# Layer 1's attention weights: the division by the row sums moves from VectorE into the transpose on TensorE

## The chip, the cores and the metric

The kernel runs on one core of a Trainium2 chip. The metric is the device time of one execution in microseconds (us). Before the change three runs took 2331.3, 2332.67 and 2340.88 us, so the median is 2332.67 us. One more execution was recorded by the hardware profiler and gave all the rows below.

## The reference

The reference is a two-layer trunk on 1024 tokens of width 1024 in float32. Layer 0 has differential attention beside a convolution module, layer 1 has a state-space block beside multi-head latent attention, and each layer ends in a gated feed-forward part. The change touches the attention of layer 1 alone:

```python
def block(i, qb):
    sc = jnp.einsum('bqhd,bkhd->bhqk', qb, k, preferred_element_type=f32) * scale
    p = jax.nn.softmax(jnp.where(chunk_causal_mask(i, s), sc, -jnp.inf), axis=-1)
    return jnp.einsum('bhqk,bkhd->bqhd', p.astype(v.dtype), v)
```

There are six heads, `q` and `k` have 128 + 64 columns, `v` has 128, and the mask lets a query see all keys up to the end of its own chunk of 64. The softmax divides each row of exponentials by its sum.

## The kernel before

Layer 1's attention is `attn1` (from L966 on). It loops over six heads `h` and, in each, two halves `hf` of 512 queries. For each (head, half) `sm1` makes the weights and, one step later, `pv1` multiplies them with the values. So the order in which the work is written is: weights of step n, then (in the first half of a head) the loads and splits of the next head, then values of step n-1.

`sm1` works through four query blocks `jj` of 128 rows. A block has n = 128 to 1024 keys, because of the causal mask: half 0 has blocks of 128 to 512 keys and half 1 blocks of 640 to 1024. TensorE makes the scores in PSUM (`pss`, five products for each bank of 512 keys, L1038). Then `softmax_exp` follows: VectorE masks a corner (L344) and copies the negated scores to SBUF while it takes their extreme (L345), ScalarE takes the exponential in place and its row sum `sm` (L346). Then VectorE takes the reciprocal of the sum (L1041) and multiplies the block's weights by it, in place (L1042).

`pv1` calls `pv`, which layer 0 uses too. For each block `i` of 128 keys it transposes up to four 128x128 blocks of weights on TensorE into a PSUM tile `trp` (L365). ScalarE rounds them to the high part of `pt` (L369), VectorE takes the rest as the low part (L370), and three products per key block go into `po` (L115). GpSimd clears a corner of `pt` once in each `pv` (L368). A `pv` of half 0 has 10 transposed blocks and one of half 1 has 26, so the six heads have 6 x 36 = 216.

Around this, GpSimd splits the next head's operands (`bl`, L977, four of 128x1024 for each head), ScalarE makes their high parts (L976), and 192 products of the output projection (`psw`, L115 out of `w_out_first`) stand at the end of the program text as work without a hurry. The program is written with a tile framework: a planner simulates the whole kernel with its own costs and fixes the order of the instructions on every engine from that, so what stands late in the text can be issued early where an engine would be idle. Each engine then runs its list in order and waits at semaphores. Buffers: `pss` has two, `trp` two, `pt` three, the weights `wt` one for each half.

Of the kernel before, what the change touches and what calls it, by code (L numbers as in the profile page):

```python
# [10 lines left out]
F32 = mybir.dt.float32  # L11
# [3 lines left out]
ALU = mybir.AluOpType  # L15
# [5 lines left out]
P = 128  # L21
# [14 lines left out]
class Trunk:  # L36
# [315 lines left out]
            r.append((b, max(w, 256)))  # L352
        return r

    def pv(self, hf, Wt, offs, V, pool):
        nc = self.nc
        o = self.pp.tile([P, HALF], F32, tag="o", name="po", bufs=1)
        ni = 4 * hf + 4
        for i in range(ni):
            j0 = max(0, i - 4 * hf)  # L360
            lo = min(j0 * P, 256)
            pt = pool.tile([P, 2, HALF], F32R, tag="pt", name="pt", bufs=3)
            tr = self.pp.tile([P, HALF], F32, tag="tr", name="trp")
            for jj in range(j0, 4):
                nc.tensor.transpose(tr[:, jj * P:(jj + 1) * P], Wt[:, offs[jj] + i * P:offs[jj] + (i + 1) * P], self.ident)  # L365
            v = slice(j0 * P, HALF)
            if j0 * P > lo:
                nc.gpsimd.memset(pt[:, :, lo:j0 * P].bitcast(F32), 0.0)  # L368
            nc.scalar.copy(pt[:, 0, v], tr[:, v])  # L369
            nc.vector.tensor_tensor(pt[:, 1, v], tr[:, v], pt[:, 0, v].bitcast(F32), op=ALU.subtract)  # L370
            self.mm3(o[:, lo:HALF], (V[0][:, i, :], V[1][:, i, :]), (pt[:, 0, lo:HALF], pt[:, 1, lo:HALF]), i == 0, i == ni - 1)
        return o
# [648 lines left out]
    def sm1(self, h, hf, ops, V, pool):  # L1021
        nc = self.nc
        qh, ql, kh, kl, rh, rl, mr = ops
        scale = 192 ** -0.5
        tot = sum((4 * hf + jj + 1) * P for jj in range(4))
        Wt = pool.tile([P, tot], F32, tag=f"w{hf}", name="wt", bufs=1)
        offs, off = [], 0
        for jj in range(4):
            j = 4 * hf + jj
            n = (j + 1) * P  # L1030
            js = slice(j * P, (j + 1) * P)
            mx = self.small.tile([P, 1], F32, tag="mx1", name="mx1")
            sm = self.small.tile([P, 1], F32, tag="sm1", name="sm1")
            ps = self.pp.tile([P, S], F32, tag="big", name="pss")
            for b0, bw in self.banks(n):
                ks = slice(b0, b0 + bw)
                for a, b, first, last in ((qh, kh, True, False), (qh, kl, False, False), (ql, kh, False, False), (rh, mr, False, False), (rl, mr, False, True)):
                    nc.tensor.matmul(ps[:, ks], a[:, js], b[:, ks], start=first, stop=last)  # L1038
            w = Wt[:, off:off + n]
            self.softmax_exp(ps, n, mx, scale, w, sm)  # L1040
            nc.vector.reciprocal(sm, sm)  # L1041
            nc.vector.tensor_scalar(w, w, sm, None, op0=ALU.mult)  # L1042
            offs.append(off)
            off += n
        return h, hf, Wt, offs, V

    def pv1(self, st, Y0, Y1, pool):
        h, hf, Wt, offs, V = st
        o = self.pv(hf, Wt, offs, V, pool)
        dst = Y0[:, 2 + h, :] if h < 2 else Y1[:, h - 2, :]  # L1050
        self.nc.scalar.copy(dst[:, hf * HALF:(hf + 1) * HALF], o)

# [480 lines left out]
```

## Time and profile before

| what | before |
|---|---|
| median of three runs | 2332.67 us |
| profiled execution, its own time | 2335.67 us |
| profiled execution, span from first to last instruction | 2333.9 us |
| TensorE busy | 2155.4 us, 92% |
| VectorE busy | 1583.1 us, 68% |
| GpSimd busy | 1275.4 us, 55% |
| ScalarE busy | 945.6 us, 41% |
| mean granted TensorE clock | 0.970 |

The attention of layer 1 lies between about 1366 and 1590 us of the span. A TensorE matmul's end is modelled, so its duration holds pipeline latency; what one costs in a stream is the distance from its start to the next start. A float32 product is recorded as two matmuls where the operation is an ordinary one, and a transpose as one. "Granted clock" 1.00 is the 2.4 GHz level of TensorE, 0.50 the 1.2 GHz level.

### The profile page before, as it was taken

How to read it: one execution, taken by the hardware profiler on the slowest of the kernel's cores; microseconds unless marked ns; L12 is line 12 of the kernel's file. 1: busy time of each engine (PE TensorE's matmuls, PEld its weight loads, DVE VectorE, ACT ScalarE, POOL GpSimd, SP SyncE). 2: the span in 40 equal slices, each digit the busy share in tenths (PEclk: the TensorE clock that was granted, in tenths of full speed). 3: DMA queues.
4: the chain of work that ended last, by engine and by line, in shares of the span. 5: the costliest groups of instructions: out<-in, count | busy, mean ns of one | idle time of the engine just before them, and what ended most of it. 6: DMA issues, size and time to landing. Idle time of an engine off the chain costs nothing.

```text
span 2333.9 us, 27188 instructions
## 1 busy us (share of the span) xinstructions
PE 2155.4 (92%) x9684; PEld 1744.8 (75%) x9684; DVE 1583.1 (68%) x2175; ACT 945.6 (41%) x1413; POOL 1275.4 (55%) x740
## 2 busy tenths in 40 slices
PE   7999888888999999799979888999899999989997
PEld 5887667677788878578758667877688888867876
DVE  6859567689747865487874478756964444437778
ACT  5554556454222322333344346654532323224332
POOL 4997202135665566687654455421565656558864
PEclk9999999999999999899989998999899999999999
DMA  5134673244232333645442674324432323255444
GB/s 207 67 109 140 169 201 113 89 155 129 92 118 97 123 129 109 213 161 163 137 154 75 198 224 137 118 79 161 136 124 75 131 73 131 73 181 186 156 129 143
DMA packets 150664, 315.33 MB, mean 135 GB/s; under 512 B 20225, under 2 KB 43905, under 8 KB 150529
## 3 DMA queue, kind: packets, MB, share of 16 engines
q1 hardware_dynamic: 150528, 313.60, 41.6%
q8 instruction: 76, 1.25, 0.2%
q14 instruction: 60, 0.48, 0.1%
HBM read 214.39 MB, written 96.01 MB: 133 GB/s over the span
## 4 chain that ended last, share of the span: by engine, by line
PE 68%; DVE 13%; DMA 6%; issue 5%; POOL 4%; ACT 3%; SPq 1%; POOLq 0%; DVEq 0%; ACTq 0%
PE b L115 30%; PE psd L115 13%; PE psw L115 6%; PE psc L115 5%; PE psq L115 3%; PE po L115 2%; PE pss L1038 2%; POOL wl L1123 2%; PE trp L365 1%; DVE hl L1253 1%; DVE acc L1271 1%; DMA bm<-k_s 1%; PE psv L115 1%; PE psu L115 1%; DMA hr<-l_h_s 1%
## 5 line engine op out<-in xcount | busy, mean ns | idle before, releaser
L1123 POOL TENSOR_TENSOR wl<-raw,wh 128x1024 fp32r<-128x1024 f32 (+1 forms) x238 | 621.3, 2616 | 399.0 <-ACT wh L1121 387.1
L115 PE MATMUL b<-T,wh 128*128 128x512 f32 x1408 | 438.6, 393 | 3.1 <-DVE F L1172 3.1
L1121 ACT CAST wh<-raw 128x1024 fp32r<-128x1024 f32 (+1 forms) x238 | 241.9, 1023 | 430.3 <-PE b L115 266.1
L115 PE MATMUL b<-B,wh 128*128 128x512 f32 x1056 | 335.2, 398 | 13.8 <-DVE c L1163 10.4
L115 PEld LDWEIGHTS b<-T,wh 128*128 128x128 f32 x1408 | 263.9, 188 | 63.1 <-issue 3.7
L115 PE MATMUL psd<-wh,hh 128*128 128x512 f32 x616 | 248.3, 404 | 42.3 <-ACT hh L1252 20.3
L115 PE MATMUL b<-T,wl 128*128 128x512 f32 x704 | 276.6, 393 | 2.3 <-POOL wl L1123 2.1
L115 PEld LDWEIGHTS b<-B,wh 128*128 128x128 f32 x1056 | 201.6, 191 | 60.3 <-ACT B L1089 7.0
L115 PE MATMUL psd<-wl,hh 128*128 128x512 f32 x616 | 245.9, 400 | 0.0
L115 PE MATMUL psd<-wh,hl 128*128 128x512 f32 x616 | 234.5, 400 | 2.2 <-DVE hl L1253 2.2
L1271 DVE TENSOR_TENSOR acc<-acc,psd 128x512 f32<-128x512 f32 (+1 forms) x208 | 178.1, 884 | 73.1 <-PE psd L115 73.1
L115 PE MATMUL b<-B,wl 128*128 128x512 f32 x528 | 209.4, 397 | 4.2 <-POOL wl L1123 4.2
L115 PE MATMUL psw<-wh,jt 128*128 128x512 f32 x512 | 175.5, 408 | 17.1 <-ACT jt L488 9.6
L1172 DVE TENSOR_TENSOR p<-p,b 128x1024 f32<-128x1024 f32 (+1 forms) x88 | 83.5, 950 | 138.1 <-PE b L115 128.1
L1252 ACT CAST hh<-hr 128x1024 fp32r<-128x1024 f32 (+1 forms) x84 | 82.2, 980 | 233.9 <-PE psd L115 200.3
L115 PEld LDWEIGHTS psd<-wh,hh 128*128 128x128 f32 x616 | 118.8, 193 | 76.4 <-ACT hh L1252 26.3
L1253 DVE TENSOR_TENSOR hl<-hr,hh 128x1024 fp32r<-128x1024 f32 (+1 forms) x84 | 148.8, 1775 | 17.5 <-DMA hr<-l_h_s 10.8
L115 PEld LDWEIGHTS b<-T,wl 128*128 128x128 f32 x704 | 132.1, 188 | 33.8 <-POOL wl L1123 3.9
L91 POOL TENSOR_TENSOR wl<-raw,wh 128x1024 fp32r<-128x1024 f32 x48 | 120.9, 2531 | 58.0 <-ACT wh L89 57.8
L115 PEld LDWEIGHTS psd<-wh,hl 128*128 128x128 f32 x616 | 118.6, 193 | 30.9 <-DVE hl L1253 3.9
L115 PEld LDWEIGHTS psd<-wl,hh 128*128 128x128 f32 x616 | 118.8, 193 | 26.0
L1173 DVE TENSOR_TENSOR raw<-raw 128x1024 f32<-128x1024 f32 x66 | 103.7, 1571 | 41.3 <-POOL wl L1123 40.2
(386 smaller groups left out, 4305.2 us busy)
## 6 DMA issues: line engine op xcount, KB each, us to landing
raw<-in_l_gu_dram SPq DMA_DIRECT2D x96, 512.0 KB, 3.6
hr<-l_h_s SPq DMA_DIRECT2D x70, 512.0 KB, 3.7
raw<-in_l_dn_dram SPq DMA_DIRECT2D x48, 512.0 KB, 3.8
l_h_s<-F SPq DMA_DIRECT2D x66, 256.0 KB, 2.2
raw<-in_w_in_dram SPq DMA_DIRECT2D x27, 512.0 KB, 3.5
l_h_s<-c SPq DMA_DIRECT2D x44, 256.0 KB, 2.0
l_h_s<-p SPq DMA_DIRECT2D x44, 256.0 KB, 2.5
raw<-in_l_w_out_dram SPq DMA_DIRECT2D x16, 512.0 KB, 3.7
```

Of the source, the lines that this page charges most:

```text
L91: nc.gpsimd.tensor_tensor(lo, raw, hi.bitcast(F32), op=ALU.subtract)
L115: mm = lambda *t, **k: self.nc.tensor.matmul(*t, skip_group_check=go, **k)
L365: nc.tensor.transpose(tr[:, jj * P:(jj + 1) * P], Wt[:, offs[jj] + i * P:offs[jj] + (i + 1) * P], self.ident)
L1038: nc.tensor.matmul(ps[:, ks], a[:, js], b[:, ks], start=first, stop=last)
L1121: nc.scalar.copy(hi[:, 0:n], r[:, 0:n])
L1123: nc.gpsimd.tensor_tensor(lo[:, 0:n], r[:, 0:n], hi[:, 0:n].bitcast(F32), op=ALU.subtract)
L1172: add = lambda o, a, b: v.tensor_tensor(o, a, b, op=ALU.add)
L1173: sub = lambda o, a, b: v.tensor_tensor(o, a, b, op=ALU.subtract)
L1252: nc.scalar.copy(hi[:, 0:n], r[:, 0:n])
L1253: v.tensor_tensor(lo[:, 0:n], r[:, 0:n], hi[:, 0:n].bitcast(F32), op=ALU.subtract)
L1271: v.tensor_tensor(dst, dst, ps, op=ALU.add)
```

## The change

The four row sums of a (head, half) go into the columns of one tile, so that one reciprocal serves the four blocks. The multiplication on VectorE is gone. Instead GpSimd makes a tile `dg` of four 128x128 diagonal matrices (identity times the reciprocals), and `pv` puts that in the place of the identity: the transpose becomes an ordinary float32 matrix product of the weights with the diagonal, which transposes and scales at once. Layer 0 still calls `pv` without `dg` and keeps its transposes.

```diff
+    def diag(self, r):
+        d = self.tmp.tile([P, 4, P], F32, tag="t", name="dg")
+        idb = self.ident.rearrange("p (o c) -> p o c", o=1).to_broadcast([P, 4, P])
+        self.nc.gpsimd.tensor_tensor(d, idb, r.rearrange("p (j o) -> p j o", o=1).to_broadcast([P, 4, P]), op=ALU.mult)
+        return d
+
-    def pv(self, hf, Wt, offs, V, pool):
+    def pv(self, hf, Wt, offs, V, pool, dg=None):
...
             for jj in range(j0, 4):
-                nc.tensor.transpose(tr[:, jj * P:(jj + 1) * P], Wt[:, offs[jj] + i * P:offs[jj] + (i + 1) * P], self.ident)
+                t, w = tr[:, jj * P:(jj + 1) * P], Wt[:, offs[jj] + i * P:offs[jj] + (i + 1) * P]
+                if dg is None:
+                    nc.tensor.transpose(t, w, self.ident)
+                else:
+                    nc.tensor.matmul(t, w, dg[:, jj, :], start=True, stop=True)
...
+        sums = self.small.tile([P, 4], F32, tag="sm1", name="sm1")
         for jj in range(4):
...
-            sm = self.small.tile([P, 1], F32, tag="sm1", name="sm1")
...
-            self.softmax_exp(ps, n, mx, scale, w, sm)
-            nc.vector.reciprocal(sm, sm)
-            nc.vector.tensor_scalar(w, w, sm, None, op0=ALU.mult)
+            self.softmax_exp(ps, n, mx, scale, w, sums[:, jj:jj + 1])
             offs.append(off)
             off += n
-        return h, hf, Wt, offs, V
+        nc.vector.reciprocal(sums, sums)
+        return h, hf, Wt, offs, V, self.diag(sums)
 
     def pv1(self, st, Y0, Y1, pool):
-        h, hf, Wt, offs, V = st
-        o = self.pv(hf, Wt, offs, V, pool)
+        h, hf, Wt, offs, V, dg = st
+        o = self.pv(hf, Wt, offs, V, pool, dg)
```

## Rows read from the trace of the kernel before

**Rows 1.** The page: busy time by engine; granted TensorE clock in 40 slices.

```profile
PE 2155.4 (92%) x9684; PEld 1744.8 (75%) x9684; DVE 1583.1 (68%) x2175; ACT 945.6 (41%) x1413; POOL 1275.4 (55%) x740
PEclk9999999999999999899989998999899999999999
```

**Rows 2.** Busy time by stretch: start:end, length, engines, granted clock, DMA.

```profile
1366.00:1400.00 34.00, 27.64 (x134) 21.29 (x133) 23.59 (x52) 22.09 (x39) 23.78 (x15) 1.00 0.56 170
1400.00:1447.00 47.00, 40.27 (x189) 33.81 (x187) 41.24 (x74) 29.92 (x52) 29.61 (x14) 0.82 0.54 155
1447.00:1564.00 117.00, 116.01 (x625) 98.75 (x625) 70.81 (x177) 65.29 (x132) 29.85 (x18) 1.00 0.26 84
1564.00:1590.00 26.00, 20.59 (x97) 16.50 (x96) 17.00 (x32) 13.06 (x27) 8.19 (x6) 0.87 0.52 160
...
1427.30:1441.00 13.70, 10.74 (x38) 9.54 (x39) 11.76 (x21) 10.30 (x21) 13.70 (x7) 0.50 0.72 203
1574.10:1580.90 6.80, 6.11 (x23) 5.45 (x24) 3.47 (x8) 2.77 (x6) 0.00 (x0) 0.50 0.78 265
```

**Rows 3.** What TensorE waited for, 1366 to 1590: us, times, longest.

```profile
PE pss L1038 <- DVE wt L345: 4.6, 6, 2.1
PE po L115 <- DVE pt L370: 3.5, 1, 3.5
PE trp L365 <- DVE pt L370: 2.0, 1, 2.0
PE trp L365 <- DVE wt L1042: 1.9, 3, 0.7
```

**Rows 4.** Groups by line, 1366 to 1590: busy us, mean ns, idle before.

```profile
L977 POOL TENSOR_TENSOR bl<-rawb,bh 128x1024 fp32r<-128x1024 f32 x20 | 51.7, 2608 | 41.5 <-ACT bh L976 41.5
L1042 DVE TENSOR_SCALAR wt<-wt,sm 128x128 f32<-128x128 f32 (+7 forms) x48 | 50.3, 1051 | 1.0
...
L365 PE MATMUL trp<-ident,wt 128*128 128x128 f32 x216 | 39.1, 290 | 4.8 <-DVE pt L370 2.0 <-DVE wt L1042 1.9 <-ACT wh L89 0.8
...
L1041 DVE RECIPROCAL sm<-sm 128x1 f32<-128x1 f32 x48 | 7.4, 157 | 3.7 <-ACT wt L346 3.5
...
L284 POOL TENSOR_TENSOR rw<-rw,ropetab 128x512 f32<-128x512 f32 x3 | 4.0, 1343 | 0.0
```

**Rows 5.** Line 1042 by itself: duration ns, shortest, median, longest.

```profile
L1042 DVE TENSOR_SCALAR wt<-wt,sm x48: 285/679/2785, 1376.8 to 1575.2; 128x128 f32<-128x128 f32 x6, 128x256 f32<-128x256 f32 x6, 128x384 f32<-128x384 f32 x6, 128x512 f32<-128x512 f32 x6
```

**Rows 6.** The transposes of line 365 by stretch: length, TensorE busy (count).

```profile
1400.00:1447.00 47.00, 8.90 (x44) 6.49 (x44) 0.82 0.54 155
1447.00:1564.00 117.00, 19.62 (x122) 15.18 (x122) 1.00 0.26 84
1564.00:1590.00 26.00, 6.91 (x35) 5.04 (x33) 0.87 0.52 160
```

**Rows 7.** Timeline of TensorE: start us, us; four transposes between products.

```profile
1450.29 0.60 PE L365 MATMUL trp<-ident,wt 128*128 128x128 f32 x4
1450.65 0.47 PE L115 MATMUL psw<-wh,jt 128*128 128x512 f32 x1
1450.96 0.39 PE L115 MATMUL psw<-wl,jt 128*128 128x512 f32 x1
```

**Rows 8.** Timeline of TensorE: ordinary float32 products of the state-space block.

```profile
1361.26 0.39 PE L772 MATMUL psY<-UT,T 128*128 128x128 f32 x2
...
1361.93 0.39 PE L772 MATMUL psY<-UT,T 128*128 128x128 f32 x2
```

**Rows 9.** Timeline of VectorE at two stalls of TensorE.

```profile
1427.14 3.92 DVE L1042 TENSOR_SCALAR wt<-wt,sm 128x640 f32<-128x640 f32 x2
...
1569.50 2.79 DVE L1042 TENSOR_SCALAR wt<-wt,sm 128x768 f32<-128x768 f32 x1
```

**Rows 10.** Timeline of GpSimd: the splits of one head's operands.

```profile
1498.42 10.41 POOL L977 TENSOR_TENSOR bl<-rawb,bh 128x1024 fp32r<-128x1024 f32 x4 [7.75 <-ACT bh L976]
```

**Rows 11.** The chain that ended last, 1340 to 1700: start, us, what.

```profile
1392.96 4.10 DMA zt<-z_s
```

## The prediction

> **What bounds the kernel now.** I read the page first: TensorE is busy 92% of the span, VectorE 68%, and the granted clock stands at nine tenths or more in most slices, with one dip of 0.8 where layer 1's attention lies [rows 1]. That says who is scarce on average, not in the stage that changes, so I cut that stage (1366 to 1590 us) into four stretches [rows 2]. In the long third one TensorE works 116.0 of 117 us at full clock, because the planner fills it with output projection products. The other three are different: TensorE is idle 6.4 us in the first, 6.7 in the second, 5.4 in the fourth, together with the third's 1.0 19.5 us, and in parts of the second and the fourth its clock is at the lower level of 1.2 GHz (13.7 and 6.8 us long, with TensorE working 10.7 and 6.1 of them).
>
> Then the list of what TensorE waited for: 12.0 us are waits for VectorE [rows 3], although little of it names line 1042 itself. VectorE takes its list in order, and 50.3 us of that list are the 48 multiplications of line 1042, the longest at 2.8 us where the shortest takes 0.29 [rows 4, 5]. At the two worst stalls they stand in front: 3.92 us for two just ahead of the 2.1 us wait for line 345, and 2.79 us for one ahead of the 3.5 us wait for line 370 [rows 3, 9]. So the stage is bound by TensorE for half its length and, at its two ends, by VectorE's line 1042.
>
> **What is removed.** 48 multiplications, 50.3 us of VectorE, and 36 of 48 reciprocals, 36 x 0.157 = 5.7 us [rows 4]. This counts on the path only where TensorE waits for it, which I price by stretch below. In the third stretch VectorE is busy 70.8 of 117 us [rows 2], and nearly nothing comes back there.
>
> **What is added on TensorE.** 216 transposes become 216 ordinary float32 products. A transpose costs 0.110 us in a stream: four of them between two 512-column products take from 1450.29 to 1450.96, which is 0.67, less one such product of about 0.23 (the distance of two neighbours), so 0.44 for four [rows 7]. An ordinary float32 product of the same shape stands in the state-space block, as two records for each: from 1361.26 to 1361.93, three products in 0.67, so 0.223 each [rows 8]. The difference is 0.113 us, times 216 is 24.5 us. The bounds: not below zero, since it is the same shape through the same weight load and more passes; upwards, if each of the 72 groups of products also pays 0.1 us where it meets products of another kind, 7 us more, 31.7. I take 24.5, because in rows 8 three kinds of operands follow each other without such a price.
>
> **A rule against the change.** The Trainium skill, "TensorE: Matmul & The Clock Gate", Terms, says that the transpose mode is four times faster for float32. By that an ordinary product would cost 0.44, the sum would be 0.33 x 216 = 71 us in place of 24.5, and the time about 2391. Rows 7 and 8 show a factor of two; this is a rival with a small chance.
>
> **What is added on GpSimd.** 12 products of 128x512. The nearest row is 1.34 us for the same size with two plain inputs [rows 4]; the trace has no such product with repeated inputs. Bounds: 0.6 us, if it went at half of that, and 2.6 us, if it took as long as a product of twice the size [rows 4]. I take 1.3, which makes 16 us in all, on an engine that is busy 91.4 of the stage's 224 us (the sum of its column in the first four of rows 2). Off the path this costs nothing as long as the weights of a step wait for the next step's scores anyway: one step's scores and fill lie between. If that cover is gone, each late product costs TensorE its delay.
>
> **What is moved and what waits.** The first transpose of a step now waits for the fourth exponential, one reciprocal and `dg`; before, the first ones needed only their own block, but a key block's tile is complete only with the fourth. Behind the reciprocal on VectorE wait the next step's lines 344 and 345; behind `dg` on GpSimd wait the splits of the next head (line 977, four in a row take 10.4 us [rows 10]), the corner clearing of line 368 and the weight splits of the output projection, and for these TensorE waits. I take zero for that, with a bound of 2.6 us (one split) at each of the 12. No DMA is added or moved in the text; the planner may shift any.
>
> **The sum, by stretch.** Products by stretch are 44, 122 and 35, the remaining 15 are in the first [rows 6].
> - First: +15 x 0.113 = 1.7, and less idle time at line 1042. Both vanish in front of the state-space output that lands at 1397 [rows 11], where TensorE waits in any case. 0.
> - Second: +44 x 0.113 = 5.0. The 2.1 us wait goes, and about 0.5 more of line 345's total [rows 3]. Of the 5.4 us lost to the lower clock (half of 10.7 us of work [rows 2]) I take half back, 2.7, since the other idle time ahead of it stays. -0.3.
> - Third: +122 x 0.113 = 13.8, less 0.6 of its 1.0 us of idle time. +13.2.
> - Fourth: +35 x 0.113 = 4.0. The 3.5 us wait goes; what is late next is `dg`, 1.3 us after the last exponential in place of a multiplication. Of 3.1 us lost to the lower clock half comes back, 1.5. -1.0.
>
> Together +11.9 us on the profiled execution's own 2335.7 us (its span is 2333.9), so 2347.6. That execution lies 3.0 us over the median of the runs shown, 2332.7; against the median it is 2344.5, and I write 2344, slower by 0.5%.
>
> **The rivals.**
> - *Nothing is given back.* The planner fills with other work wherever VectorE held TensorE up, so idle time and the lower clock turn up elsewhere, and only the first stretch absorbs its share. Then 24.5 - 1.7 = 22.8: 2355.5. For it: 116.0 of 117 us busy in the third stretch. Against: in the fourth no fill is left, there are 5.4 us of idle time [rows 2]. It decides if less than 5 us of idle time and clock come back.
> - *It is not slower.* All 12.0 us of waits for VectorE [rows 3] and all of the 8.4 us lost to the lower clock (half of 10.7 and 6.1) come back: 24.5 - 1.7 - 12.0 - 8.4 = +2.4, so 2335. For it: 56 us less on VectorE, a third of its load in the stage. Against: waits for ScalarE and for VectorE's other lines would take over part of it. It decides from about 16 us given back; to be faster by over 0.5% it would need more than the trace has to give, unless the planner's new order does better elsewhere.
> - *GpSimd is late.* `dg` stands behind a split or behind the corner clearing in GpSimd's list, and TensorE runs out of work before it. At six of the twelve steps by one split of 2.6 us: 15.6 more on top of my sum, 2360. For it: the splits come four in a row [rows 10]. Against: a whole step lies between. It decides as soon as TensorE's waits name the new line for over 3 us.
> - *Fourfold products*, the rule above: 2391.
>
> **Chances and range.** Mine 0.42, with a range of its own from 2338 to 2351 (the bounds of clock and idle time given back, 4 us to one side, and 7 us for switching to the other); nothing given back 0.22; not slower 0.17; GpSimd late 0.12; fourfold 0.03; a new order that gains elsewhere 0.04. A measurement of this kernel can tell about 0.5% from no change, which is 11.7 us, 2321 to 2344.3. My case lies on that edge and splits about evenly. Slower: 0.21 + 0.21 + 0.12 + 0.03, less a little of each for a luckier planner, 0.53. Same: 0.21 + 0.14 + 0.05 = 0.40. Faster: 0.03 of the not-slower case and 0.04 of the new order, 0.07. The range for 8 in 10 goes from 2330 to 2361, from below the not-slower case to just over the late GpSimd.
>
> **What would show it.** In the changed profile: 432 records of ordinary 128x128 products at line 365's place, in pairs 0.223 us apart from one product to the next; line 1042 gone and VectorE in the stage at some 100 us in place of 152.6 (the column's sum in rows 2); 12 products on GpSimd of about 1.3 us; TensorE's waits for VectorE down from 12 to about 5 us; the last transposes some 3 us sooner after the last scores; the clock back to 1.00 in one of the two stretches. I am wrong in the price if the pairs are not 0.223 us apart, wrong in the cover if TensorE waits for `dg`, and wrong in what returns if the stage's idle time is not cut by 6 to 9 us.

## The result and the profile after

The changed kernel takes 2364.26 us (median of four runs, 2361.63 to 2366.66) where the kernel before, on the same chip, takes 2334.48 us. The ratio is 1.0122 with an interval of 1.0105 to 1.0140: slower by 28.5 us (24.5 to 32.7); the two medians by themselves lie 29.8 us apart. The forecast was +11.9 us, and the time lies 3 us above its range. The profiled execution has 2363.47 us of its own and a span of 2361.7 us.

Lines of the page (busy time; the clock in 40 slices), against [rows 1]:

```profile
PE 2186.5 (93%) x9900; PEld 1778.6 (75%) x9900; DVE 1552.5 (66%) x2091; ACT 947.0 (40%) x1413; POOL 1285.3 (54%) x752
PEclk9999989999999999899989989999999999999999
```

TensorE has 216 records and 31.1 us more, VectorE 30.6 us less. In the clock row the digit 8 at the 25th slice stands a slice earlier, the one at the 29th, behind the attention, is gone and a new one stands at the 6th, long before it. From the page alone nobody would say that 28 us were lost, let alone where.

The stage runs from the last product of the state-space block (`psY`) to the last product with the values (`po`). Its row of the kernel before (columns: start:end, length, busy TensorE, weight loads, VectorE, ScalarE, GpSimd with their counts, granted clock, DMA share, GB/s):

```profile
1365.40:1588.00 222.60, 204.30 (x1039) 170.15 (x1037) 151.95 (x331) 129.78 (x246) 91.43 (x51) 0.95 0.39 122
```

The same columns for the changed kernel, the whole stage and then four stretches that answer to [rows 2]:

```profile
1369.00:1612.50 243.50, 226.18 (x1255) 196.41 (x1253) 105.96 (x247) 131.67 (x246) 98.13 (x62) 0.96 0.35 109
1369.00:1403.00 34.00, 28.33 (x138) 22.90 (x136) 15.72 (x37) 22.03 (x37) 23.98 (x16) 0.91 0.55 171
1403.00:1455.00 52.00, 42.95 (x218) 37.88 (x219) 25.66 (x54) 29.84 (x52) 25.58 (x15) 0.86 0.40 112
1455.00:1589.00 134.00, 132.08 (x764) 116.08 (x762) 52.56 (x133) 68.65 (x134) 40.98 (x27) 1.00 0.26 83
1589.00:1615.00 26.00, 24.14 (x145) 20.65 (x146) 12.71 (x27) 12.25 (x26) 7.59 (x7) 1.00 0.49 157
```

The stage grew from 222.6 to 243.5 us, by 20.9. VectorE lost 46.0 us there (151.95 to 105.96), and yet TensorE's idle time, the length less its busy time, is nearly what it was: 18.3 us before, 17.3 after. The fourth stretch is healed (1.9 us idle, clock 1.00, against 5.4 us and 0.87), the first and second are not: 5.7 and 9.1 us idle, clocks 0.91 and 0.86. So the puzzle is why 46 us less on VectorE freed next to nothing.

The other 7 us of these two executions lie outside: 3.6 ahead of the stage (it begins at 1369.0 against 1365.4) and 3.3 behind it. Ahead of it the engines' lists are the same, and yet the twelve profiles of this case begin the stage anywhere from 1360.8 to 1371.5; a second profile of the same changed kernel began it at 1365.1. So a few us outside the stage, between two single profiles, are not read here as an effect.

What TensorE waited for in the stage (us in all, times, longest), against [rows 3]:

```profile
PE po L115 <- DVE pt L380: 4.0, 3, 3.6
PE pss L1048 <- POOL bl L987: 3.7, 2, 2.7
PE po L115 <- ACT pt L379: 2.6, 4, 1.3
PE pss L1048 <- ACT bh L986: 1.9, 1, 1.9
PE psgl L115 <- DVE zl L800: 1.8, 1, 1.8
PE psw L115 <- DVE jt L499: 1.7, 1, 1.7
```

No row names the new tile. On the lines that [rows 3] counts, the waits for VectorE fell from 12.0 to 4.6 us (4.0, and 0.6 for line 345). With all of VectorE's lines (`zl` and `jt` too) they fell from 13.5 to 8.1 us. In their place stand the operand splits, which GpSimd (`bl`) and ScalarE (`bh`) make for the next head: 5.6 us, where it had been 1.5.

The changed groups in the stage (busy us, mean ns of one | idle time before and what ended it), against [rows 4]:

```profile
L375 PE MATMUL trp<-dg,wt 128*128 128x128 f32 x432 | 60.2, 278 | 0.0
L375 PEld LDWEIGHTS trp<-dg,wt 128*128 128x128 f32 x432 | 58.7, 195 | 3.6 <-POOL dg L358 0.2
...
L986 ACT CAST bh<-rawb 128x1024 fp32r<-128x1024 f32 x21 | 20.9, 1043 | 2.9 <-PE po L115 2.4 <-DMA rawb<-k_s 0.5
...
L358 POOL TENSOR_TENSOR dg<-ident,sm 128x512 f32<-128x512 f32 x12 | 13.9, 1161 | 23.3 <-DVE sm L1053 23.2
```

432 records are the 216 products, two for each. The tile costs GpSimd 13.9 us, less than forecast. Its row ends in 23.2 us during which GpSimd stood waiting for the sums, in five of twelve places; in six of the other seven the tile waited for GpSimd.

What one product costs is read from the starts in TensorE's timeline (start us, us, what), as in [rows 7]:

```profile
1465.69 1.05 PE L375 MATMUL trp<-dg,wt 128*128 128x128 f32 x8
1466.49 0.47 PE L115 MATMUL psw<-wh,jt 128*128 128x512 f32 x1
1466.81 0.39 PE L115 MATMUL psw<-wl,jt 128*128 128x512 f32 x1
```

From 1465.69 to 1466.81 pass four products and one of 512 columns: 1.12 - 0.23 = 0.89, or 0.223 each. That is the price forecast.

Now one tile in detail, the one of head 0's upper half. First ScalarE, with the last exponential of that half:

```profile
1394.85 1.15 ACT L346 ACTIVATE wt<-wt,mx 128x1024 f32<-128x1024 f32 x1
```

Then GpSimd:

```profile
1392.19 2.38 POOL L987 TENSOR_TENSOR bl<-rawb,bh 128x1024 fp32r<-128x1024 f32 x1 [3.29 <-ACT bh L986]
1394.50 0.32 POOL L378 MEMSET pt<- 128x256 f32 x1
1394.77 7.01 POOL L987 TENSOR_TENSOR bl<-rawb,bh 128x1024 fp32r<-128x1024 f32 x3
1401.72 2.03 POOL L358 TENSOR_TENSOR dg<-ident,sm 128x512 f32<-128x512 f32 x1
```

And TensorE, with the first products that use the tile:

```profile
1408.87 1.95 PE L375 MATMUL trp<-dg,wt 128*128 128x128 f32 x16
```

The weights are done at 1396.0. On GpSimd three splits, begun at 1394.8, stand ahead of the tile; it starts at 1401.7, 5.7 us after the weights, and ends at 1403.8. TensorE's products follow at 1408.9, because the order written ahead has other work in front: 77 score products and 12 products of the gate (`psgl`) come between the start of the stage and this point, where the kernel before had 61 and 3. TensorE doesn't wait for the tile by name; its own list was laid out around a late tile.

### The profile page after: what moved, and what is told of

Its sections match the earlier page's. It is cut to its first block, busy times and chain, and to the rows that moved or that the text cites. A ratio compares the mean times of both kernels' runs of the same rounds, so it can differ in the third digit from the quotient of the medians.

```text
span 2361.7 us, 27576 instructions
## 1 busy us (share of the span) xinstructions
PE 2186.5 (93%) x9900; PEld 1778.6 (75%) x9900; DVE 1552.5 (66%) x2091; ACT 947.0 (40%) x1413; POOL 1285.3 (54%) x752
## 4 chain that ended last, share of the span: by engine, by line
PE 69%; DVE 12%; DMA 6%; issue 5%; POOL 4%; ACT 4%; SPq 1%; POOLq 0%; DVEq 0%; ACTq 0%
PE b L115 30%; PE psd L115 13%; PE psw L115 6%; PE psc L115 5%; PE psq L115 3%; PE po L115 3%; PE pss L1048 2%; POOL wl L1132 2%; PE trp L375 2%; DVE hl L1262 1%; ACT junk L106 1%; PE pss L462 1%; DMA bm<-k_s 1%; PE psv L115 1%; DMA hr<-l_h_s 1%
## 5 line engine op out<-in xcount | busy, mean ns | idle before, releaser
L115 PE MATMUL b<-B,wh 128*128 128x512 f32 x1056 | 336.8, 400 | 17.1 <-DVE c L1172 8.5
L1262 DVE TENSOR_TENSOR hl<-hr,hh 128x1024 fp32r<-128x1024 f32 (+1 forms) x84 | 154.3, 1840 | 17.2 <-ACT hh L1261 17.2
```

Source lines behind the costliest of these rows:

```text
L115: mm = lambda *t, **k: self.nc.tensor.matmul(*t, skip_group_check=go, **k)
L1262: v.tensor_tensor(lo[:, 0:n], r[:, 0:n], hi[:, 0:n].bitcast(F32), op=ALU.subtract)
```

## The experiments

Theory 1 was that the tile is off the path (within 3 us) and the products alone make the loss. Theory 2 was that the tile is late; the later expectations call it theory A. All times are medians, compared with runs of the kernel before on the same chip; the last column is the ratio's difference from 1, times 2334 us, and differences between kernels are taken from it (the ratio is not quite that of the medians: in e9 these lie 3.0 us apart, in e1 27.7). e2, e4 and e10 leave the division out, so they only measure and are no versions to use.

| kernel | division | into `trp` | ratio to before | us |
|---|---|---|---|---|
| changed, repeated (e1) | tile, GpSimd | product | 1.0116 (1.0103 to 1.0129) | +27.1 |
| e2 | none | transpose | 0.9957 (0.9944 to 0.9969) | -10.0 |
| e3 | VectorE, as before | product | 1.0066 (1.0052 to 1.0079) | +15.4 |
| e4 | none | product | 1.0052 (1.0037 to 1.0067) | +12.1 |
| e5 | tile, VectorE | product | 1.0046 (1.0034 to 1.0058) | +10.7 |
| e6 | tile, ScalarE | product | 1.0058 (1.0044 to 1.0072) | +13.5 |
| e7 | tile, GpSimd; splits on VectorE | product | 1.0082 (1.0069 to 1.0095) | +19.1 |
| e8 | on the result, rows late | transpose | 1.0027 (1.0015 to 1.0039) | +6.3 |
| e9 | on the result, rows early | transpose | 1.0003 (0.9988 to 1.0019) | +0.7 |
| e10 | none, tile made and unused | product | 1.0044 (1.0033 to 1.0056) | +10.3 |

**First round: which part costs what.** e1 is the changed kernel without an edit.

> The changed kernel once more, unaltered. Of the 27.8 us between the two profiles only 20.9 lie in the attention of layer 1; 3.6 stand before it, where the order of the instructions is the same, and 3.4 behind it. Theory (price of the products, little given back): the attention again takes 243 to 245 us from the last state-space product to the last value product, and the time is 23 to 26 us over the kernel before. Rival (the change also costs something outside its stage, some 7 us): again 3 to 4 us late at the start of the stage and 28 to 30 us in all.

2361.55 us (2358.83 to 2361.96): the loss is there again, and the +27.1 us lie between the two ranges. Its stage repeats the first profile's 243.5 us within 0.5 and begins no later than in the kernel before:

```profile
1365.10:1608.10 243.00, 224.76 (x1255) 195.00 (x1253) 106.34 (x247) 131.73 (x246) 99.13 (x63) 0.96 0.35 109
```

e2 takes the division out of the kernel before:

```diff
             self.softmax_exp(ps, n, mx, scale, w, sm)
-            nc.vector.reciprocal(sm, sm)
-            nc.vector.tensor_scalar(w, w, sm, None, op0=ALU.mult)
```

> The kernel before with its transposes, but without the reciprocals and multiplications of lines 1041 and 1042: the weights are not divided at all. This is what the removal alone gives back. My prediction credited about 11 us: 2323. Theory (the planner had filled TensorE's time while VectorE was busy, and other waits take the place): 0 to 5 us, 2329 to 2334.

2323.92 us. The removal by itself is worth 10.0 us; the forecast had given back 10.9 (22.8 - 11.9). Its stage:

```profile
1365.40:1576.40 211.00, 199.06 (x1039) 166.62 (x1037) 100.47 (x235) 130.10 (x246) 89.66 (x51) 0.97 0.41 129
```

222.6 became 211.0 us, 11.6 less. Idle time fell from 18.3 to 11.9 us, and the clock rose from 0.95 to 0.97.

e3 keeps VectorE's division and puts products with the identity in the transposes' place; e4 does both edits:

```diff
-                nc.tensor.transpose(tr[...], Wt[...], self.ident)
+                if prod:
+                    nc.tensor.matmul(t, w, self.ident, start=True, stop=True)
+                else:
+                    nc.tensor.transpose(t, w, self.ident)
...
-        o = self.pv(hf, Wt, offs, V, pool)
+        o = self.pv(hf, Wt, offs, V, pool, True)
```

> The kernel before with its division on VectorE, but layer 1's transposes are ordinary float32 products with the identity. This is the products' price alone: by 0.113 us times 216, 24.5 us, less 1.7 absorbed, so 2356 to 2359 if the median before is 2334. Rival (the new tile and its place on GpSimd make a good part of the loss): the price of the products shows only partly on the path, under 18 us, so below 2352.

> Products with the identity and no division at all: the changed kernel without reciprocals and without the tile of diagonals. Against the changed kernel it gives the price of that tile and of the wait for it. Theory (off the path): within 3 us of the changed kernel. Rival (GpSimd is late, its list is shifted): 6 to 10 us below the changed kernel.

e3 takes 2350.26 us, e4 2346.13. So the products by themselves cost 15.4 us with the division in place: the rival's case (under 18), not the 22 to 25 of the theory. The stages of e3 and of e4 (two views):

```profile
1367.00:1603.20 236.20, 221.33 (x1255) 192.38 (x1253) 149.59 (x331) 130.66 (x246) 89.08 (x50) 0.98 0.34 107
```

```profile
1371.50:1597.50 226.00, 217.93 (x1254) 188.93 (x1253) 99.75 (x235) 129.86 (x246) 83.44 (x49) 1.00 0.35 110
```

e3's stage is 13.6 us longer than that of the kernel before: its idle time fell from 18.3 to 14.9 us and its clock rose from 0.95 to 0.98, although VectorE still divides. e4 has 8.1 us of idle time and a clock of 1.00 from end to end. Against e2 its stage is 15.0 us longer and the time 22.1; the part of that which lies outside the stage isn't explained here. Against the kernel before, e4 loses 12.1 us, almost the +11.9 of the forecast, but its stage is only 3.4 us longer (226.0 against 222.6). The changed kernel differs from e4 only by twelve reciprocals, twelve tiles and the products' use of them, and is 15.0 us slower (+27.1 against +12.1). Theory 1 fell here, and the loss is larger than theory 2 had expected.

**Second round: is it the tile's place?** e5 moves the tile to VectorE:

```diff
-        self.nc.gpsimd.tensor_tensor(d, idb, ...)
+        self.nc.vector.tensor_tensor(d, idb, ...)
```

> The changed kernel, but the twelve diagonal tiles are made by VectorE instead of GpSimd; nothing else differs. Theory A (the tile stands behind the next head's four splits in GpSimd's list, so the products of the first groups start late, the operand buffers of the next heads come free late, and the chain of heads is stretched): VectorE has no splits to finish first, so the first 40 products of head 0's upper half start about 28 to 31 us after the last Y product instead of 39.8, and the time falls from about 2361.5 to 2346-2353 (the run with products and no tile had 2346.1, and twelve tiles of 0.7 to 1.3 us each come back on VectorE). Theory B (the wait for the fourth sum before any product, whatever engine makes the tile): the products start as late as with GpSimd, and the time stays at 2357 or above.

2346.74 us (2345.17 to 2347.84), as theory A said. Its stage, then VectorE at the tile that was late before, then TensorE's products with it (three views of the same kernel):

```profile
1367.80:1594.20 226.40, 218.55 (x1254) 190.44 (x1253) 116.15 (x259) 130.39 (x246) 88.21 (x51) 0.99 0.36 113
```

```profile
1394.71 0.18 DVE L1053 RECIPROCAL sm<-sm 128x4 f32<-128x4 f32 x1 [2.98 <-ACT wt L346]
1394.92 1.10 DVE L358 TENSOR_TENSOR dg<-ident,sm 128x512 f32<-128x512 f32 x1
```

```profile
1397.21 1.63 PE L375 MATMUL trp<-dg,wt 128*128 128x128 f32 x8
```

The tile is begun 0.3 us after the last exponential instead of 5.7 us, and the products come 29.4 us after the stage's start instead of 39.9. Idle time is 7.9 us where the changed kernel has 17.3. The stage is 17.1 us shorter and the time 16.4, for a change of one engine's name.

e6 puts the tile on ScalarE, as four activations:

```diff
+        for j in range(4):
+            self.nc.scalar.activation(d[:, j, :], self.ident, AF.Copy, scale=r[:, j:j + 1])
```

> The changed kernel, but each diagonal tile is made by four ScalarE activations of one 128x128 block (the identity, scaled by the reciprocal) instead of one GpSimd instruction. Theory A (the tile's place in GpSimd's list): the time falls to 2347-2356, a little more than with VectorE, since 48 more instructions of about 0.25 us stand on ScalarE, which also has the exponentials. Theory B (the wait for the fourth sum, on any engine): 2357 or above.

2348.65 us (2344.58 to 2354.85). Its price is on the row (48 pieces, 15.4 us), and still it is 13.6 us below e1. So what decides is less what the tile costs than which list it stands in.

```profile
L358 ACT ACTIVATE dg<-ident,sm 128x128 f32<-128x128 f32 x48 | 15.4, 393 | 1.1 <-DVE sm L1053 1.0
```

e7 leaves the tile on GpSimd and moves the splits away:

```diff
-            eng = nc.gpsimd if h else nc.vector
+            eng = nc.vector
```

> The changed kernel with its diagonal tiles left on GpSimd; moved is what stands ahead of them there, the lower-half splits of layer 1's later heads, to VectorE (twenty instructions). Theory A (the tile waits behind the splits): the first tile is made within 2 us of the fourth sum, the products of head 0's upper half start 28 to 32 us after the last Y product, and the time falls to 2344-2356; how far depends on what the splits cost VectorE. Theory B (the wait for the fourth sum): 2357 or above, and the first products no earlier than 36 us. If GpSimd's list matters but VectorE's does too, the tile is early and the time still near 2360.

2355.84 us, at the upper end of theory A's range: 8.0 us below e1, half of what e5 recovers. GpSimd now waits for the sums at this tile, and TensorE's products come 34.3 us after the stage's start (two views):

```profile
1397.58 1.04 POOL L358 TENSOR_TENSOR dg<-ident,sm 128x512 f32<-128x512 f32 x1 [5.54 <-DVE sm L1053]
```

```profile
1402.84 1.36 PE L375 MATMUL trp<-dg,wt 128*128 128x128 f32 x9
```

The tile is early, the products are 2 us later than A allowed, and the twenty splits cost VectorE 1.22 us each, 24.4 us in all. The run has a mixed answer: it supports that the splits were in the way, and suggests that they are in the way on VectorE too.

e8 looks for another place for the division: the result of a half is multiplied by the inverted sums, put across the partitions by four transposes.

```diff
...
-        self.nc.scalar.copy(dst[:, hf * HALF:(hf + 1) * HALF], o)
+        rs = self.rstd_b(sums)
+        self.nc.vector.tensor_tensor(dst[:, hf * HALF:(hf + 1) * HALF], o, rs, op=ALU.mult)
```

> The kernel before, but layer 1's attention weights aren't divided at all: the four sums of a group are kept, inverted in one instruction and put across the partitions by four transposes, and the 128x512 result of the group is multiplied by them on VectorE as it is copied out of PSUM (in place of ScalarE's copy). The transposes stay transposes. If the gain of leaving out the division (2323.9 against 2333.8) is VectorE's time between the exponentials and the transposes, it is kept but for 48 more transposes (48 x 0.11 = 5.3 us at most, on TensorE) and 12 multiplications at the end of a group: 2324-2331, faster than both kernels. If the chain at a group's end (sums, transposes, copy, multiplication) is on the path twelve times, it gives back up to 12 x 2 us: 2335-2348.

2342.97 us (2337.74 to 2348.86): the second case, 6.3 us slower than before. TensorE's longest wait in it, and its stage (two views):

```profile
PE pss L1038 <- ACT bh L976: 6.8, 2, 3.9
```

```profile
1369.80:1592.50 222.70, 206.48 (x1087) 172.45 (x1085) 109.51 (x258) 131.61 (x247) 85.23 (x50) 0.96 0.39 119
```

**Third round.** e9 is e8 with the call of `rstd_b` moved ahead of the products with V.

> The late division again, with one call moved: the four transposes that put a group's inverted sums across the partitions, and ScalarE's copy of them, stand before the group's products with V instead of behind them, so that the multiplication which empties the result bank can start with the last product. If what the late division gave back (2343.0 against 2323.9 with no division at all, of which about 5 us are the 48 transposes) is the chain at a group's end, in which the result bank waits for transposes, copy and multiplication, the time falls to 2328-2336, level with or a little below the kernel before. If it is the order that the additional work gives the lists of ScalarE and VectorE elsewhere, it stays at 2339-2346.

2337.01 us (2329.92 to 2349.66). Against e8 that is 5.6 us less (to some 5 us by the intervals), and the wait above has gone to 0.4 us (two views, the wait and the stage):

```profile
PE pss L1038 <- ACT bh L976: 0.4, 1, 0.4
```

```profile
1371.10:1586.10 215.00, 203.71 (x1088) 169.59 (x1087) 108.39 (x259) 131.22 (x248) 84.31 (x50) 0.98 0.39 123
```

In the stage e8 has 11.7 us more than e2, and 7.7 of them went with the one moved call, so there the greater part of what the late division costs is the chain at a half's end. In device time it is less clear: e9 is still 10.7 us above e2, of which the 48 more transposes are priced at 5.3. The time is a microsecond above the range of the first case, not different from the kernel before; of the versions that divide, none beats that kernel.

e10 is the most direct test. The tile is made as in the changed kernel, and nobody uses it:

```diff
-                    nc.tensor.matmul(t, w, dg[:, jj, :], start=True, stop=True)
+                    nc.tensor.matmul(t, w, self.ident, start=True, stop=True)
```

> The changed kernel with its twelve diagonal tiles still made on GpSimd, from the same sums and at the same place, but the products take the identity instead: the weights are not divided. So no product waits for a tile, while GpSimd's list is as before. Theory A (the products wait for a tile that is late): the time falls to that of the run without tiles, 2345-2350. Theory C (the tile, itself waiting for the fourth sum, holds up what stands behind it on GpSimd, the splits and the clearing of corners, whoever uses it): 2356 or above.

2345.20 us (2340.14 to 2352.02). GpSimd, then TensorE:

```profile
1388.47 9.36 POOL L987 TENSOR_TENSOR bl<-rawb,bh 128x1024 fp32r<-128x1024 f32 x4
1397.79 2.02 POOL L358 TENSOR_TENSOR dg<-ident,sm 128x512 f32<-128x512 f32 x1
```

```profile
1393.20 1.26 PE L375 MATMUL trp<-ident,wt 128*128 128x128 f32 x6
```

The tile stands behind its four splits just as in the changed kernel, and nearly as late: it starts 4.4 us after the last exponential. But the products no longer need it. They start 4.6 us before it, 26.9 us into the stage, and the stage is:

```profile
1366.30:1592.20 225.90, 218.86 (x1254) 190.31 (x1252) 102.98 (x247) 130.77 (x246) 98.40 (x63) 0.99 0.36 111
```

Same work on TensorE, the same GpSimd load as the changed kernel (98.4 and 98.1 us), and a stage 17.6 us shorter: 10.3 us of it idle time (17.3 to 7.0), 7.3 us busy time at the higher mean clock (0.99 against 0.96). So it isn't GpSimd's load, nor what stands behind the tile, but the products' dependence on a late tile.

## Why the prediction was wrong, point by point

**Right: the product's price in a stream. Too large: what it costs on the path.** Forecast was 0.113 us over a transpose, 24.5 us for 216, and 22.8 of it on the path. The pair distance in the changed kernel is 0.223 us, and no product cost fourfold. But with the division in place (e3) the products cost 15.4 us, in the stage 13.6, and without it (e4 against e2) 15.0 in the stage: part of their time came back as clock and idle time, with no relief of VectorE.

**Right: the relief.** Forecast 10.9 us given back. Measured are 10.0 in e2, and in the stage 11.6; with products in the transposes' place (e3 to e4) it is 10.2 in the stage, though only 3.3 in device time, to some 5 us by the intervals.

**Right in its total, for another kernel, and partly by luck: their sum.** +11.9 forecast; e4, e5 and e10, in which no product waits for a late tile, have +12.1, +10.7 and +10.3. The forecast put all of this into the stage, and there the three are only 3.3 to 3.8 us longer than the kernel before. The rest of their loss lies ahead of the stage and behind it, where nothing was changed, and stays unexplained.

**Wrong: the tile's place.** The step that failed is under "What is added on GpSimd": "Off the path this costs nothing as long as the weights of a step wait for the next step's scores anyway", and with it, in the fourth stretch, "what is late next is `dg`, 1.3 us after the last exponential". Measured is 16.4 us (+27.1 against +10.7 for the same tile on VectorE) or 16.8 (against +10.3 for the tile unused), each to some 4 us by the intervals. Two things were wrong in the step:
- The forecast knew of four splits in a row, 10.4 us [rows 10], but let them wait behind the tile. In the first four heads the tile of the upper half falls due among the splits of the next head and waits behind those that stand ahead of it. In the changed kernel's trace it started 5.7, 4.6, 3.8, 3.8, 0.4 and 0.4 us after the last exponential of the six upper halves.
- The cover was taken for free time. The scores of the next step do lie between, but the step's own end matters to others. The weights have one buffer for each half, so line 345 of the next head's upper half can only write when the last product with the tile has read this head's. In the changed kernel it starts within 0.3 us of that product's end in all five places, and so it does in e5, only sooner. The first place, in the changed kernel and in e5:

```profile
1430.98 0.47 PE L375 MATMUL trp<-dg,wt 128*128 128x128 f32 x2
1431.49 0.82 DVE L345 TENSOR_SCALAR_CACHE_REDUCE wt<-pss 128x640 f32<-128x640 f32 x1
```

```profile
1419.75 0.38 PE L375 MATMUL trp<-dg,wt 128*128 128x128 f32 x2
1420.17 0.82 DVE L345 TENSOR_SCALAR_CACHE_REDUCE wt<-pss 128x640 f32<-128x640 f32 x1 [0.23 <-PE trp L375]
```

ScalarE's operands (`bh`) wait for the products with the values too (2.4 us for `po` in its row), but the kernel before has 4.6 us of the same waits. ScalarE's group of four high parts that begins 68.5 us into the changed kernel's stage begins at 57.7 in e5. The last exponentials of the upper halves of heads 0 to 5 come at these times after the stage's start:

| | head 0 | 1 | 2 | 3 | 4 | 5 |
|---|---|---|---|---|---|---|
| changed | 27.0 | 74.5 | 115.8 | 157.4 | 194.9 | 230.1 |
| e5 | 26.8 | 64.9 | 98.7 | 137.1 | 172.6 | 210.8 |

They start level; 9.6 us are lost by head 1, 20.3 by head 3, 22.3 by head 4. Some of that is made up by the end. Part of the idle time shows up as waits for `bl` and `bh`. That the delay travels from head to head through these buffers is read from the rows; no run gave the weights or the operands a second buffer.

The other zero of the forecast, "I take zero for that, with a bound of 2.6 us (one split) at each of the 12", for what waits behind the tile, held: e10 has the tile in GpSimd's list and is not slower than e4, which has none (+10.3 against +12.1).

**The right rival with the wrong sign to look for.** "GpSimd is late" had the mechanism and, by another count (six steps by one split), nearly the price: 15.6 us on top of the sum. It was to be decided by "TensorE's waits name the new line for over 3 us". They name it for 0.2 us. Since the order of every list is written ahead, a late input doesn't appear here as a wait for it: the consumer is listed later, other work is pulled ahead of it, and the lost time appears where that other work would have been. How much of the 16 us is the order written ahead and how much the chip's own delay was not separated.

**A wrong rival whose sign came true.** "Nothing is given back" asked for 22.8 us and for less than 5 us of idle time and clock returned. The changed kernel's stage is 20.9 us longer, so only 3.6 of the 24.5 us came back. From the changed kernel's stage alone this rival would have looked right; e2, e5 and e10 show that the return is there as soon as no product waits for a late tile.

**The signs listed at the end.** Held: 432 records, 0.223 us, VectorE at 106.0 us in the stage, twelve tiles (1.16 us), the waits for VectorE at 4.6 us on the lines that were counted, the last transposes 2.4 us sooner after the last scores (15.4 against 17.9 us), the clock back to 1.00 in the fourth stretch. Failed: idle time cut by 1.0 instead of 6 to 9 us. It was named as the sign against the return; in e10, without the late tile, the cut is 11.3 us.

## What to carry to other kernels

A new instruction's price includes its place: before putting it on the engine with the lowest load, list what that engine has in a row at the moment the input is ready, and count all of it. When the list is ordered ahead, don't look for a wait that names the new line; compare the times at which consumers start, and confirm with a kernel in which the new result is made but not used. And a division that leaves a busy engine isn't free elsewhere: here 10 us came back, and twice as many TensorE records took 22 or, with the division kept, 15.

## What the runs showed of the hardware

On GpSimd and VectorE the same 128x512 tile has very different durations, by what the other of the two engines is doing. On GpSimd it took 1.04 us at the median and 2.03 at 1401.72, when VectorE was in a subtraction with two 128x1024 inputs (line 800); that one, beside a split and the tile, took 2.98 us from 1399.88, where in e7, without splits on GpSimd, an equal one took 1.23:

```profile
1399.88 2.98 DVE L800 TENSOR_TENSOR zl<-zt,zh 128x1024 fp32r<-128x1024 f32 x1 [2.88 <-ACT zh L798]
```

In e5, on VectorE, it took 0.69 us in stretches without splits on GpSimd and 2.65 at 1505.26, in the middle of four splits that GpSimd ran from 1500.25 to 1510.16:

```profile
1477.15 0.69 DVE L358 TENSOR_TENSOR dg<-ident,sm 128x512 f32<-128x512 f32 x1
...
1505.26 2.65 DVE L358 TENSOR_TENSOR dg<-ident,sm 128x512 f32<-128x512 f32 x1
```

Which of the two starts first decides here which one pays. Seven of e5's twelve tiles start while a split runs on GpSimd, and each ends 0.55 us after that split's end: the one above at 1507.91, the split at 1507.36. The tile at 1408.95 starts just ahead of a split; it keeps its 0.69 us, and the split takes 2.85 where most take 2.4:

```profile
1408.95 0.69 DVE L358 TENSOR_TENSOR dg<-ident,sm 128x512 f32<-128x512 f32 x1
```

```profile
1409.03 2.85 POOL L987 TENSOR_TENSOR bl<-rawb,bh 128x1024 fp32r<-128x1024 f32 x1 [1.86 <-ACT bh L986]
```

The Trainium skill, "GPSIMD Engine Reference", Specifications, says that GpSimd shares its SBUF interfaces with VectorE and contends with VectorE's instructions that have two SBUF inputs; these rows agree.

The second surprise was the clock: more work on TensorE went with a better clock. The stage of e4 has 24.4 us more of work than the one of e2 (216 x 0.113) and a mean granted clock of 1.00 against 0.97, with 8.1 us of idle time against 11.9. e3 and the kernel before differ in the same way, 0.98 against 0.95. So some of what the products cost came back as clock and idle time, which the forecast had expected from the relief of VectorE alone. With the late tile most of it is gone: 0.96, and 17.3 us of idle time.
